# Attention filler: Q and K of a seventh pair computed in the seven-product phase, 13 filler steps a block, the output product one block sooner

## The chip, the cores and the metric

The kernel runs on one core of one Trainium2 chip. The metric is the device time of one execution in microseconds (us), the median of several runs. All of the arithmetic is float32 kept to float32 accuracy by splitting operands into a high and a low part, as told below.

## The reference, cut to what matters

A two-layer decoder trunk over 1024 positions of width 1024: layer 0 mixes with a short gated convolution, layer 1 with dilated attention of 16 heads of 64, and each is followed by a SwiGLU feed-forward. The change touches layer 1's attention only:

```
def dilated_attention_mixer(h, w_qkv, w_out, rel_bias):
    qkv = (h @ w_qkv).reshape(bsz, seq, 3, N_HEADS, HEAD_DIM)
    q, k, v = qkv[:, :, 0], qkv[:, :, 1], qkv[:, :, 2]
    for window, dilation in BRANCHES:                 # (128,1), (512,4), (2048,16)
        o, l = dilated_branch(q, k, v, rel_bias, window, dilation)
        ...
    alpha = jax.nn.softmax(jnp.stack(lses, axis=0), axis=0)
    o = jnp.sum(alpha[..., None] * jnp.stack(outs, axis=0), axis=0)
    return o.reshape(bsz, seq, D_MODEL).astype(h.dtype) @ w_out
...
            x = x + dilated_attention_mixer(h, attn_w_qkv[j], attn_w_out[j], rel_bias)
```

The kernel merges the three branches of a head into one softmax with one common maximum. The result is the same sum.

## The kernel before, in words

**Matmuls.** Every 32-bit operand of the projections is kept as two parts, high and low (`split`, lines 143 and 144: ScalarE rounds the high part, VectorE subtracts to get the low part), and every product of two 128-row tiles is three matmuls (high by high, high by low, low by high). The large products run in a Strassen form: a unit of 2 by 2 blocks takes seven products instead of eight (`Strassen`; its matmuls are lines 572 to 574). A unit needs sums of weight blocks first (`combo`, line 191), sums of partial results behind (`save`, line 578, on ScalarE; `add`, line 582, on VectorE), and 7 x 4 x 3 = 84 matmuls of 512 columns for two weight tiles over all 1024 positions. The plain form (`projections`, its matmuls in `product`, lines 371 to 373) takes 2 x 2 x 8 x 3 = 96 matmuls for the same.

**The seven-product phase.** `QueryKey` computes Q and K for the first `QK_PAIRS` = 6 of the 8 pairs of heads: one unit a pair, in the order of `unit_order`. Each of the four results of a unit goes through `emit` (lines 1140 to 1149): VectorE scales it, ScalarE rounds the high part, VectorE makes the low part, and GpSimd's queue writes both to `kq` in DRAM. Behind the phase come the value tiles of group 0 (`value_tiles`, lines 1512 to 1517: matmuls of 256 columns, 24 to a bank).

**The attention phase.** There are 17 calls of `slot`, called blocks 0 to 16 here. Block n does the scores of head n (`scores`, matmuls lines 1569 and 1570; VectorE adds the bias, lines 1580 to 1611, and keeps the maximum, `m`, lines 1594 to 1620), then the maximum over all partitions on GpSimd (`mb`, line 1623), then the softmax (`softmax`: VectorE subtracts, line 1631; ScalarE takes the exponentials, line 1632), and the product of the exponentials of head n-1 with its values (`values`, matmuls line 1642; ScalarE then copies the two result banks, lines 1665 and 1666). Up to block LAG = 13 ("lagged") the first half of a block interleaves scores with filler, and the second half interleaves the values of head n-1 with filler; the softmax of head n is issued at i = 3 of the second half's eight rounds. From block 14 on, the values of head n-1 run beside the scores of head n.

**Filler.** `fill()` is a generator of independent matmul work, and a block takes a fixed number of its steps, 15: 8 in the first half (4 in block 0, other numbers from block 14 on), the rest spread over the second. The list `FILL` sets its order: values of group 1 and 2, the plain projections of pairs 6 and 7, values of group 3; then `out_product`, the attention's output product over the first four pairs (`AO` = 4), which adds into `X`. A group of value tiles is 40 steps (one step in five only copies a bank and has no matmul; the others have six matmuls of 256 columns), a pair's projections 36 steps (32 with three matmuls of 512 columns), the output product 64 steps (three matmuls of 512 columns each). `take` splits the next weight slabs a little ahead: in `value_tiles` at the steps where j = 1 and b4 is 1 or 2, in `projections` when the second part is taken.

**Operands of the output product.** `load_attended(range(AO))` reads the first four pairs' results (`oin`) back from DRAM through the SyncE queue ahead of block LAG-1 = 12, and the generator `halves` splits one pair into `first` each time it is advanced: in block 12's second half, at i = 4 to 7, behind the softmax. With 15 steps a block, the 192 steps of values and projections end at step 12 of block 12, so the output product begins in the same block.

**Order and space.** The order on each engine is the order of the program (no scheduler). All engines' waits follow from the tiles they share. Full-size tiles come from one pool of 41 pages, 8 PSUM banks serve all matmuls, and the values of a pair are held in a single tile, `vx`.

Of the kernel before, what the change touches and what calls it, by code (L numbers as in the profile page):

```python
# [20 lines left out]
H = 16  # L21
# [20 lines left out]
FFN_PAIRS, FFN_CHUNK = 9, 3  # L42
CONV_PAIRS, CONV_CHUNK, CO = 0, 1, 4
CONV, QK = "conv", "qk"
QK_PAIRS = 6
PAGES = 41
SOFT = 4
FIN0 = 2
AO_WIDE = 5
AO = 4  # L50
LAG = 13
FILL = (("v", 0), ("v", 1), ("v", 2), ("qk", 6), ("qk", 7), ("v", 3))
DEEP_ORDER = (1, 2, 5, 6, 7, 3, 4)


# [44 lines left out]
def trunk(ctx: ExitStack, tc: tile.TileContext, x, gains_in, cwi, ck, cwo, wqkv, wo, relb,  # L100
# [8 lines left out]
    def page(name, dt=F32):  # L109
        return pages.tile([128, 1024], dt, name=name, tag="page", bufs=PAGES)  # L110
# [228 lines left out]
    def add_ffn(i):  # L339
        add_units(i, FT, lambda u, n: (wg, wu)[u % 2][i][u - u % 2 + n])  # L340
        add_down(i, wd[i], FFN_PAIRS, FFN_CHUNK, ("d", i))
# [3 lines left out]
    add_ffn(0)  # L345
    add_units(QK, QK_PAIRS, lambda u, n: wqkv[(KT, 0)[n] + u])
    for kind, g in FILL:
        if kind == "v":
# [47 lines left out]
    class Norm:  # L396
        def __init__(self, gi):
            self.g = gi
            self.h = {}
            self.acc = self.rstd = None  # L400
            self.put_off = None
# [720 lines left out]
    class QueryKey(Conv):  # L1122


        def __init__(self, norm):
            Strassen.__init__(self, QK, norm, QK_PAIRS, 0, 1, 0, None)
            self.waiting, self.ready, self.begun = [], False, iter(())
# [332 lines left out]
    def load_bias(h):  # L1460
        t = scope["pool"].tile([128, L1 + L2], F32, name="bias", tag="bias", bufs=2)
        base = tables.offset + h * G3
        nc.sync.dma_start(t[:, 0:L1], bass.AP(tensor=tables.tensor, offset=base, ap=[[1, 8], [A1, 16], [1, L1]]))
        nc.sync.dma_start(t[:, L1:L1 + L2], bass.AP(tensor=tables.tensor, offset=base + G0,
                                                    ap=[[1, 32], [A2, 4], [1, L2]]))
        return t
# [8 lines left out]
    def attention(norm, qk):  # L1475
# [58 lines left out]
        def load_kq(n):  # L1534

            p, a = divmod(n, 2)
            k, q = qk.kq[p, 1], qk.kq[p, 0]
            rows = lambda t, r: bass.AP(t.tensor, t.offset + r * S, [[S, 64], [1, S]])
            n0, n1 = (slice(64 * i, 64 * i + 64) for i in (a, 1 - a))
            KS[n], QS[n] = page("ka", F32R), page("qa", F32R)  # L1540
            nc.sync.dma_start(KS[n][n0].bitcast(F32), rows(k, 64 * a))
            nc.sync.dma_start(KS[n][n1].bitcast(F32), rows(k, 128 + 64 * a))
            if n <= LAG + 1 and n % 2 == 0 and n:
                load_values(p - 1)
            for m in (n0, n1):
                nc.sync.dma_start(QS[n][m].bitcast(F32), rows(q, 64 * a))
            nc.sync.dma_start(qlo[a][n0].bitcast(F32), rows(q, 128 + 64 * a))

        def classes(n):

            KC[n] = page("kca", F32R)
            for h in range(2):
                nc.scalar.activation(KC[n][:, half(h)], view(KS[n], h * HALF, [[1, 4], [4, 128]]), AF.Copy)
                yield
# [80 lines left out]
        def values(p, a, st):  # L1635
            lf, lh, ld, lp = (st[n] for n in ("lf", "lh", "ld", "lp"))
            acc = [bank(), bank()]
            kd = [[128, 4], [1, 32]]
            b1 = [[32, 16], [1, 8]]

            def mm(ih, off, dims, u, rhs, first=False, last=False):
                nc.tensor.matmul(view(acc[ih], off, dims), vx[:, u, 64 * a:64 * a + 128], rhs,  # L1642
                                 start=first, stop=last)

            for ih in range(2):
                for r4 in range(4):
                    mm(ih, r4 * 32, kd, 8 + r4, view(lf, ih * HALF + r4 * 32, kd), first=r4 == 0)
                    if r4 % 2:
                        yield
            for r4 in range(4):  # L1650
                mm(1, r4 * 32, kd, 12 + r4, view(lh, r4 * 32, kd))
                if r4 % 2:
                    yield
            for j in range(8):
                off = (j % 4) * 8
                mm(j // 4, off, b1, j, view(ld, blk(j), b1), last=False)
                if j:
                    mm(j // 4, off, b1, j - 1, view(lp, blk(j), b1), last=j % 4 == 3)
                yield
            o, z = st["o"], st["z"]  # L1660
            n0 = slice(64 * a, 64 * a + 64)
            z0 = slice(64 - 64 * a, 128 - 64 * a)
            for ih in range(2):
                s = slice(ih * HALF, (ih + 1) * HALF)
                nc.scalar.activation(z[n0, s], acc[ih][z0], AF.Ln)
                nc.scalar.activation(o[n0, s], acc[ih][n0], AF.Copy)
            yield
# [45 lines left out]
        def slot(n, dense, ndense, late=0, hook=iter(())):  # L1713

            def other(k):
                for _ in range(k):
                    next(dense, None)

            p, a = divmod(n, 2)
            if n < H:  # L1720
                new = dict(bias=bias.pop(n))
                sc = scores(p, a, new)
            else:
                sc = iter(())
            if n + 1 < H:
                load_kq(n + 1)
                bias[n + 1] = load_bias(n + 1)
            if n:
                q, b = divmod(n - 1, 2)
                if b == 0:  # L1730
                    OZ[q] = page("o"), page("z")
                old = live.pop(n - 1)
                old.update(o=OZ[q][0], z=OZ[q][1])
                pv = values(q, b, old)
            else:
                pv = iter(())
            extra = later = iter(())
            lagged = n <= LAG
            if n + 1 < H:
                later = classes(n + 1)  # L1740
            if lagged and a and p:
                ending.append(finish(p - 1))
            used = 0
            if lagged:
                for i in range(8):
                    next(sc, None)
                    if n or i % 2:
                        other(1)
                        used += 1
                    if a and ending and i == 0:  # L1750
                        run(ending.pop())
                run(sc)
            else:
                if a == 0 and not late:
                    other(1)
                    used += 1
                for i in range(8):
                    next(sc, None)
                    next(pv, None)
                    next(pv, None)  # L1760
                    if i >= late and i % 2 == 0:
                        other(1)
                        used += 1
                run(sc)
                run(pv)
                if a == 0:
                    extra = finish(p - 1)
                if a == 0 and n < H:
                    load_values(p)
            left = max(ndense - used, 0)  # L1770
            for i in range(8):
                next(pv, None)
                next(pv, None)
                if i == (2 if n > LAG + 1 else 5):
                    attended()
                if not lagged and (i < FIN0 or i > SOFT):
                    next(extra, None)
                if i in (1, 2):
                    next(later, None)
                if i == (3 if lagged else SOFT):  # L1780
                    if n < H:
                        live[n] = new
                        run(softmax(new))
                if i >= SOFT:
                    next(hook, None)
                other(left * (i + 1) // 8 - left * i // 8)
            run(pv)
            run(extra)
# [36 lines left out]
        def fill():  # L1825
            for kind, g in FILL[1:]:
                if kind == "qk":
# [6 lines left out]
        def halves():  # L1834
            for q, t in done.items():
                first[q] = split(t)
                yield

        dense = fill()
        for n in range(H):  # L1840
            if n == LAG - 1:
                done.update(load_attended(range(AO)))
            hook = halves() if n == LAG - 1 else iter(())
            slot(n, dense, 15, 3 if n == H - 2 else 0, hook)
            run(hook)
        acts.update(split_attended(load_attended(range(AO, 7))))
        ensure(ahead_ao)
        slot(H, dense, 15)
        run(dense)
        return acts  # L1850

# [39 lines left out]
    with tc.tile_pool(name="first", bufs=1) as scope["pool"]:  # L1891
# [5 lines left out]
        qk = QueryKey(norm)  # L1897
# [152 lines left out]
```

## Time and profile before

| | |
|---|---|
| median of 3 runs | 2130.8 us (2130.04 to 2131.32) |
| the profiled execution: time | 2129.8 us |
| the profiled execution: span, first to last instruction | 2128.0 us |
| granted TensorE clock, mean | 0.996 |
| TensorE matmuls (PE) busy | 2102.3 us, 99% |
| TensorE weight loads (PEld) busy | 1806.5 us, 85% |
| VectorE (DVE) busy | 1739.8 us, 82% |
| ScalarE (ACT) busy | 1015.7 us, 48% |
| GpSimd (POOL) busy | 234.4 us, 11% |

How to read it: the span is the profiled execution without what lies around it, 1.8 us here. Times in rows are us from the span's start. A matmul's duration in a row overlaps the next one's, so the pitch from start to start is what a matmul costs when TensorE is fed; a busy PE is therefore not yet a fed PE, and its waits have to be looked up. "A <- B" in a view of waits means that engine and line A sat idle until B was done. SPq is the SyncE queue, which issues the loads. Page here means one of the pool's 41 tiles; a page of the profile is named as such.

In the trace, the seven-product phase of Q and K lies at about 972 to 1087 us, block 0 begins at 1110.5, block 1 at 1122.8, block 12 at 1333.0, block 13 at 1358.3, and the last block ends at about 1436.6.

### The profile page before, as it was taken

To read this page: it belongs to the slowest core of one execution; us is meant where nothing else is said; L and a number is where in the kernel's file an instruction comes from. 1 tells how busy PE (TensorE), PEld (TensorE's weight loads), DVE (VectorE), ACT (ScalarE), POOL (GpSimd) and SP (SyncE) were. 2 spreads that over 40 slices of the span, in tenths; PEclk is the share of its full clock that TensorE was granted. 3 is DMA by queue.
4 is the path that set the end of the run, shared out by engine and by line. 5 is a ranking of instruction groups with operands and counts; after the bars stand their busy time and mean duration, and the time that the engine had idled before them with its cause. 6 is when DMAs were issued, how large, how long until landed. Compare 5 with 4: busy or idle time off the path is not lost.

```text
span 2128.0 us, 30922 instructions
## 1 busy us (share of the span) xinstructions
PE 2102.3 (99%) x11082; PEld 1806.5 (85%) x11082; DVE 1739.8 (82%) x3262; ACT 1015.7 (48%) x1861; POOL 234.4 (11%) x335
## 2 busy tenths in 40 slices
PE   9999999999999999999999999999999999999998
PEld 7888888888888888887899999888788888888887
DVE  8898769988888888878967687787998888888876
ACT  7333426443444554445545545554544444456435
POOL 1000000110101000010322322111011101001000
PEclk9999999999999999999999999999999999999999
DMA  7332642323333566351767767745223233358432
GB/s 219 94 94 70 228 134 75 104 100 109 114 101 108 162 208 211 108 168 40 250 208 186 182 182 211 216 164 152 64 85 109 101 108 114 105 195 241 157 95 79
DMA packets 141464, 300.78 MB, mean 141 GB/s; under 512 B 48188, under 2 KB 54414, under 8 KB 141312
## 3 DMA queue, kind: packets, MB, share of 16 engines
q1 hardware_dynamic: 107488, 201.94, 31.5%
q0 software_dynamic: 26192, 82.17, 11.9%
q10 hardware_dynamic: 7632, 14.70, 1.8%
q8 instruction: 88, 1.44, 0.3%
q14 instruction: 64, 0.52, 0.1%
HBM read 208.48 MB, written 82.93 MB: 137 GB/s over the span
## 4 chain that ended last, share of the span: by engine, by line
PE 85%; DVE 7%; ACT 3%; DMA 2%; issue 2%; POOL 1%; SPq 0%; DVEq 0%; ACTq 0%; POOLq 0%
PE bank L574 19%; PE bank L572 19%; PE bank L573 19%; PE bank L373 4%; PE bank L372 4%; PE bank L371 4%; PE bank L664 3%; PE bank L667 3%; PE bank L666 3%; PE bank L1642 2%; POOL mb L1623 1%; PE bank L1512 1%; PE bank L1513 1%; PE bank L1514 1%; DVE w L144 1%
## 5 line engine op out<-in xcount | busy, mean ns | idle before, releaser
L572 PE MATMUL bank<-b,w 128*128 128x512 f32 x1952 | 764.0, 391 | 2.2 <-ACT w L143 1.8
L574 PE MATMUL bank<-b,w 128*128 128x512 f32 x1952 | 762.0, 390 | 3.6 <-DVE w L144 3.5
L573 PE MATMUL bank<-b,w 128*128 128x512 f32 x1952 | 761.4, 390 | 0.4 <-DVE b L883 0.3
L574 PEld LDWEIGHTS bank<-b,w 128*128 128x128 f32 x1952 | 366.9, 188 | 83.9 <-DVE w L144 7.4
L572 PEld LDWEIGHTS bank<-b,w 128*128 128x128 f32 x1952 | 367.2, 188 | 78.9 <-ACT w L143 2.9
L573 PEld LDWEIGHTS bank<-b,w 128*128 128x128 f32 x1952 | 367.1, 188 | 76.3 <-DVE b L883 1.1
L143 ACT ACTIVATE w<-combo 128x512 fp32r<-128x512 f32 (+2 forms) x488 | 249.1, 540 | 230.2 <-DVE combo L191 213.3
L144 DVE TENSOR_TENSOR w<-combo,w 128x512 fp32r<-128x512 f32 (+2 forms) x488 | 277.7, 583 | 37.6 <-ACT w L143 36.9
L578 ACT ACTIVATE part<-bank 128x512 f32<-128x512 f32 x186 | 110.8, 596 | 390.0 <-PE bank L574 386.6
L144 DVE TENSOR_TENSOR w<-raw,w 128x512 fp32r<-128x512 f32 (+2 forms) x342 | 189.5, 576 | 37.5 <-ACT w L143 37.5
L582 DVE TENSOR_TENSOR part<-part,bank 128x256 f32<-128x256 f32 (+1 forms) x366 | 171.5, 500 | 31.1 <-PE bank L574 16.6
L143 ACT ACTIVATE w<-raw 128x512 fp32r<-128x512 f32 (+2 forms) x342 | 166.9, 530 | 44.4 <-PE bank L574 11.5
L371 PE MATMUL bank<-w_hi,w 128*128 128x512 f32 (+1 forms) x400 | 153.4, 384 | 3.8 <-ACT w_hi L143 3.7
L372 PE MATMUL bank<-w_lo,w 128*128 128x512 f32 (+1 forms) x400 | 149.8, 375 | 1.2 <-DVE w_lo L144 1.2
L373 PE MATMUL bank<-w_hi,w 128*128 128x512 f32 (+1 forms) x400 | 149.8, 375 | 0.7 <-DVE w L144 0.7
L493 DVE TENSOR_TENSOR x<-x,bank 128x512 f32<-128x512 f32 (+1 forms) x104 | 66.4, 644 | 62.6 <-PE bank L373 61.4
L802 DVE TENSOR_TENSOR x<-x,bank 128x512 f32<-128x512 f32 x136 | 93.2, 685 | 29.1 <-PE bank L574 29.1
L191 DVE TENSOR_TENSOR combo<-raw 128x512 f32<-128x512 f32 (+1 forms) x172 | 111.7, 649 | 0.0
L371 PEld LDWEIGHTS bank<-w_hi,w 128*128 128x128 f32 x400 | 75.8, 190 | 17.1 <-ACT w_hi L143 3.9
L372 PEld LDWEIGHTS bank<-w_lo,w 128*128 128x128 f32 x400 | 75.9, 190 | 14.9 <-DVE w_lo L144 2.0
L373 PEld LDWEIGHTS bank<-w_hi,w 128*128 128x128 f32 x400 | 75.6, 189 | 14.7 <-DVE w L144 1.6
L565 DVE TENSOR_TENSOR b<-hin,b 128x512 fp32r<-128x512 f32 x126 | 79.7, 689 | 9.3 <-ACT b L564 9.3
(243 smaller groups left out, 3467.1 us busy)
## 6 DMA issues: line engine op xcount, KB each, us to landing
hin<-part SPq DMA_DIRECT2D x126, 256.0 KB
raw<-in_ffn_w_gate SPq DMA_DIRECT2D x44, 512.0 KB
raw<-in_ffn_w_up SPq DMA_DIRECT2D x44, 512.0 KB
part<-sum POOLq DMA_DIRECT2D x72, 256.0 KB, 2.3
raw<-in_ffn_w_down SPq DMA_DIRECT2D x48, 384.0 KB
raw<-in_attn_w_qkv SPq DMA_DIRECT2D x27, 512.0 KB
raw<-in_conv_w_in SPq DMA_DIRECT2D x24, 512.0 KB
part<-part POOLq DMA_DIRECT2D x36, 256.0 KB, 2.4
```

The lines of the kernel that those rows point to most:

```text
L143: nc.scalar.activation(hi, src, AF.Copy)
L144: eng.tensor_tensor(out=lo, in0=src, in1=hi, op=ALU.subtract)
L191: eng.tensor_tensor(out=c, in0=a, in1=b, op=op)
L371: nc.tensor.matmul(b, whi[:, a], ahi[:, s], start=first, stop=False)
L372: nc.tensor.matmul(b, whi[:, a], alo[:, s], start=False, stop=False)
L373: nc.tensor.matmul(b, wlo[:, a], ahi[:, s], start=False, stop=last)
L572: nc.tensor.matmul(b, hi[:, a], bhi, start=start and k == 0, stop=False, skip_group_check=True)
L573: nc.tensor.matmul(b, hi[:, a], blo, start=False, stop=False, skip_group_check=True)
L574: nc.tensor.matmul(b, lo[:, a], bhi, start=False, stop=k == n - 1, skip_group_check=True)
L578: nc.scalar.activation(t, b, AF.Copy)
L582: nc.vector.tensor_tensor(out=t, in0=t, in1=b, op=ALU.add)
L802: nc.vector.tensor_tensor(out=X[n][:, half(h)], in0=X[n][:, half(h)], in1=b, op=ALU.add)
```

## The change

`QK_PAIRS` goes from 6 to 7: pair 6 becomes a seventh unit of the seven-product phase and leaves the filler. The filler loses its 36 steps (220 left of 256), and a block takes 13 steps, named `DENSE`, instead of 15. The values and projections are then 156 steps, which is 12 blocks of 13, so the output product begins with the first step of block 12. Its operands are loaded ahead of block 11 and split in block 11 (LAG-2 instead of LAG-1), at i = 0 to 3 of the second half, ahead of the softmax instead of behind it.

```
-QK_PAIRS = 6
+QK_PAIRS = 7
...
-FILL = (("v", 0), ("v", 1), ("v", 2), ("qk", 6), ("qk", 7), ("v", 3))
+FILL = (("v", 0), ("v", 1), ("v", 2), ("qk", 7), ("v", 3))
+DENSE = 13
...
                 if i in (1, 2):
                     next(later, None)
+                if i < 4:
+                    next(hook, None)
                 if i == (3 if lagged else SOFT):
                     if n < H:
                         live[n] = new
                         run(softmax(new))
-                if i >= SOFT:
-                    next(hook, None)
                 other(left * (i + 1) // 8 - left * i // 8)
...
         for n in range(H):
-            if n == LAG - 1:
+            if n == LAG - 2:
                 done.update(load_attended(range(AO)))
-            hook = halves() if n == LAG - 1 else iter(())
-            slot(n, dense, 15, 3 if n == H - 2 else 0, hook)
+            hook = halves() if n == LAG - 2 else iter(())
+            slot(n, dense, DENSE, 3 if n == H - 2 else 0, hook)
             run(hook)
         acts.update(split_attended(load_attended(range(AO, 7))))
         ensure(ahead_ao)
-        slot(H, dense, 15)
+        slot(H, dense, DENSE)
         run(dense)
```

## The prediction

> **What bounds the kernel now.** I read the page's busy times first, then busy time by stage, then TensorE's (PE's) waits in the attention blocks, then VectorE's (DVE's).
>
> ```profile
> PE 2102.3 (99%) x11082; PEld 1806.5 (85%) x11082; DVE 1739.8 (82%) x3262; ACT 1015.7 (48%) x1861; POOL 234.4 (11%) x335
> ...
> 972.00:1090.00 118.00, 116.78 (x525) 95.11 (x524) 109.50 (x171) 65.97 (x112) 23.12 (x43) 1.00 0.47 162
> 1122.80:1333.00 210.20, 207.11 (x1590) 197.56 (x1589) 160.60 (x287) 114.89 (x163) 57.05 (x52) 1.00 0.72 191
> 1333.00:1358.30 25.30, 21.11 (x151) 19.84 (x150) 16.60 (x28) 16.19 (x25) 5.95 (x6) 0.87 0.53 176
> 1348.30:1352.20 3.90, 0.21 (x2) 0.02 (x1) 1.99 (x3) 3.74 (x7) 0.00 (x0) 0.84 0.01 2
> 1352.20:1357.50 5.30, 4.79 (x14) 3.82 (x15) 3.58 (x3) 4.43 (x7) 2.17 (x4) 0.50 0.39 102
> 1358.30:1436.60 78.30, 77.53 (x496) 69.75 (x495) 62.21 (x106) 40.62 (x62) 10.79 (x5) 1.00 0.65 193
> ```
>
> The columns of a stage are its length, busy time (and count) of PE, weight loads, DVE, ACT and POOL, granted clock, DMA share, GB/s. The stages are the seven-product phase, blocks 1 to 11, block 12, a hole in it (two rows), and blocks 13 to 16. PE is busy nearly everywhere; the exception is block 12, where it is empty for 3.9 us and then at clock 0.50 for 5.3 us.
>
> ```profile
> PE bank L371 <- ACT w_hi L143: 3.7, 1, 3.7
> PE bank L1569 <- ACT o L1666: 2.7, 3, 1.1
> PE bank L372 <- DVE w_lo L144: 1.2, 2, 0.8
> PE bank L1569 <- ACT v L1517: 0.3, 1, 0.3
> ...
> 1352.24 0.79 PE L371 MATMUL bank<-w_hi,w 128*128 128x512 f32 x1 [3.72 <-ACT w_hi L143]
> 1353.50 0.79 PE L372 MATMUL bank<-w_lo,w 128*128 128x512 f32 x1 [0.47 <-DVE w_lo L144]
> 1360.06 0.50 PE L372 MATMUL bank<-w_lo,w 128*128 128x512 f32 x1 [0.77 <-DVE w_lo L144]
> ```
>
> The waits are all of PE's over blocks 0 to 16, the rest its timeline. The hole is the output product's first step (L371): its operand, split from `oin` on ACT behind the softmax, comes when PE has nothing else left to do. The other waits are for PSUM banks that ACT frees late (L1666).
>
> ```profile
> DVE lf L1631 <- POOL mb L1623: 35.3, 11, 3.5
> DVE w_lo L144 <- ACT w_hi L143: 9.3, 4, 3.5
> DVE kq_lo L1148 <- ACT kq_hi L1145: 3.6, 4, 1.3
> DVE lf L1580 <- PE bank L1570: 1.8, 3, 1.0
> DVE ld L1606 <- PE bank L1570: 0.9, 3, 0.4
> DVE lh L1589 <- PE bank L1570: 0.8, 1, 0.8
> ```
>
> These are DVE's waits in blocks 1 to 11. In 210.2 us it waits for PE only 1.8 + 0.9 + 0.8 = 3.5 us. Its other idle time is its own loop: maximum, GpSimd's reduction `mb` (about 3.2 us a block), softmax. So PE and DVE pace these blocks together, each with some 3 us of slack, and filler taken from PE is worth only as much as DVE's loop lets through. That is the main question here.
>
> **The change part by part.** The price of a matmul:
>
> ```profile
> 1430.10 0.39 PE L372 MATMUL bank<-w_lo,w 128*128 128x512 f32 x1
> ...
> 1449.82 0.39 PE L372 MATMUL bank<-o_lo,w 128*128 128x512 f32 x1
> ...
> 1343.10 0.28 PE L1514 MATMUL bank<-w_hi,b 128*128 128x256 f32 x1
> 1343.22 0.28 PE L1512 MATMUL bank<-w_hi,b 128*128 128x256 f32 x1
> ```
>
> Between the first two rows run 87 matmuls of 512 columns back to back: 19.72 / 87 = 0.227 us each. The other two give 0.12 us for 256 columns. A filler step of projections or output product is 3 x 0.227 = 0.68 us, one of values with matmuls 6 x 0.12 = 0.72 us.
>
> *1. The seventh unit* adds 84 x 0.227 = 19.0 us of PE. DVE beside it:
>
> ```profile
> L191 DVE TENSOR_TENSOR combo<-raw 128x512 f32<-128x512 f32 x7 | 4.8, 688 | 0.0
> L144 DVE TENSOR_TENSOR w<-combo,w 128x512 fp32r<-128x512 f32 x17 | 11.7, 685 | 0.1
> L582 DVE TENSOR_TENSOR part<-part,bank 128x512 f32<-128x512 f32 x10 | 6.8, 684 | 2.3 <-ACT part L578 2.3
> ...
> L144 DVE TENSOR_TENSOR w_lo<-raw,w_hi 128x1024 fp32r<-128x1024 f32 x8 | 10.7, 1361 | 9.3 <-ACT w_hi L143 9.3
> L1148 DVE TENSOR_TENSOR kq_lo<-kq,kq_hi 128x512 fp32r<-128x512 f32 x8 | 6.1, 768 | 3.6 <-ACT kq_hi L1145 3.6
> L1140 DVE TENSOR_TENSOR kq<-bank,rstd 128x512 f32<-128x512 f32 x4 | 4.2, 1052 | 0.0
> L1142 DVE SCALAR_TENSOR_TENSOR kq<-bank,rstd 128x512 f32<-128x512 f32 x4 | 2.7, 682 | 0.0
> ```
>
> (mean ns is the number after the busy time.) Four sums, seven splits, three additions, two scalings of K, two of Q and four low parts: 4 x 0.69 + 7 x 0.69 + 3 x 0.68 + 2 x 1.05 + 2 x 0.68 + 4 x 0.77 = 16.2 us, under the 19.0 of PE, so it hides. The cost is at least 19.0. It is at most about 21: DVE is busy 109.5 of 118 us in the phase, and four `b` tiles of block 8 now lie beside a whole further unit in a pool of 41, so splits may wait for a page; 2 us is my estimate, some two of the 0.69 us splits with their ACT halves. I take 19.0. The two weight loads and eight `kq` writes only move.
>
> *2. The filler* loses 32 steps with matmuls, 32 x 0.68 = 21.8 us of PE. By stage, from the step numbers (15n to 15n+14 before, 13n to 13n+12 after; four in five value steps count): block 0 loses 1.6 value steps, 1.2 us. Blocks 1 to 11 go from 74.4 value and 64 projection steps (97.1 us) to 85.6 and 32 (83.4 us), 13.7 us less. Blocks 12 to 16 lose the 9.6 value steps that spilled into block 12, 6.9 us.
>
> *3. Blocks 1 to 11, what is let through.* PE alone: 210.2 - 3.0 (bank waits) - 13.7 = 193.5. DVE alone: 210.2 - 3.5 (its waits for PE) = 206.7. It loses pair 6: four low parts, four scalings, two wide splits, 4 x 0.77 + 2 x 1.05 + 2 x 0.68 + 2 x 1.36 = 9.3, and half of the 3.6 waited for `kq_hi`. It gains the four operand splits in block 11, 4 x 1.36 = 5.4 us, of which 3.5 fill the empty wait for `mb`: 1.9 more. DVE alone is 206.7 - 9.3 - 1.8 + 1.9 = 197.5. The longer decides: DVE, 197.5, a gain of 12.7. Ends: 193.5 (gain 16.7), and 197.5 + 3.5 if DVE still waits for PE as often (gain 9.2).
>
> *4. Block 12's hole.* The operands are split a block earlier, in the wait for `mb`, before ACT's exponentials. The hole goes: 3.9 us, half of the 5.3 us at clock 0.50 (2.65), and the 0.77 wait, 7.3 in all. What is late next is the addition into `X`, which waits for its load from `spill`. The moved loads:
>
> ```profile
> 1300.01 0.54 POOL L1708 DMA_DIRECT2D odram<-o  x1 [4.54 <-DVE o L1707]
> 1297.67 0.47 SPq L1541 DMA_DIRECT2D ka<-kq  x1
> 1313.84 1.26 SPq L1531 DMA_DIRECT2D vx<-vdram  x2
> SPq L1805 <- PE bank L1570: 8.0, 1, 8.0
> ```
>
> On SyncE's queue the four `oin` loads pass ahead of head 12's `ka`, `vx`, `qa`, `ql` and bias loads (`ka` ran at 1297.67). They must wait for the fourth pair's write, issued at 1300.01, and hold that group some 5 us; but its second half of `vx` waits for head 9's values until 1313 anyway, so `qa` behind it is no later. I take nothing. On POOL only `vdram` writes come sooner. `X`'s loads (L1805) waited 8.0 us for a tile's release by the scores (L1570), in block 12's first half; they now stand ahead of it in the program, when `oin`'s four pages are free again. I take nothing.
>
> *5. The tail.* From block 14 on the values of head n-1 follow its softmax at once, and two fewer steps (1.36 us) stand between. At most that is lost again in blocks 15 and 16, 2.8 us; at least nothing. I take 0.5, since DVE is busy only 62.2 of 78.3 us in blocks 13 to 16.
>
> Sum: 19.0 - 1.2 - 12.7 - 7.3 - 6.9 + 0.5 = -8.6 us, against the profiled execution's 2129.8 (span 2128.0): 2121.2. That execution lay 1.0 below the median 2130.8, so the forecast is 2122.2.
>
> **The rivals.**
>
> *PE alone paces (chance 0.16).* DVE's waits for ACT and `mb` shrink as its load does, and part 3 gains 16.7: 2118.2. For it: in eleven blocks PE waits for banks only 3.0 us, though DVE is hardly ever ahead of it. Against it: those waits exist already, with more filler.
>
> *DVE loses more (0.16).* Weight splits now fall on steps 25, 65, 98 and 141, that is at a block's end or first step, where ACT still copies out the values' banks; DVE then stands with the next head's additions queued behind it. The worst wait of this kind is 3.5 us: 4 x 3.5 instead of 9.3 is 4.7 more: 2126.9.
>
> *Slower (0.13): bank waits that halve the clock.* The longest bank wait is 1.1 us now. Each block loses up to 1.4 us of PE work in which ACT could free the banks; if in blocks 2 to 11 lateness adds up over two or three blocks, one wait reaches the 3.7 us after which the clock fell to 0.50 in block 12. Each such hole costs 7.3, and from the second on the gain is gone: 2122.2 + 14.6 = 2136.8. The Trainium skill, "TensorE: Matmul & The Clock Gate", Part 1, states such a gate: after an idle window of about 3.4 us the clock falls to half until a busy window has passed. The rows of block 12 agree, at 3.72 us and 0.50; by that rule waits below it cost only their own length, and then this rival needs holes that no row but block 12's shows.
>
> *The hole only moves (0.08).* If `X` or a weight slab is late in block 12, PE stops there again for as long: 2122.2 + 7.3 = 2129.5, no change.
>
> **How the numbers follow.** A measurement tells about 0.2%, 4.3 us, from no change: below 2126.5 is faster. The forecast case has 0.47. Faster: 0.47 + 0.16 + half of DVE's case = 0.71; same: its other half and the moved hole, 0.16; slower 0.13. Range: 2116.0 (PE alone, with the last bank waits gone) to 2130.0 (the moved hole and half a us of unknown), which leaves out the slower case.
>
> **What the profile after would show.** Right: no PE wait on ACT `w_hi`, no stage at clock 0.50; seven units; blocks 1 to 11 in 195 to 199 us; DVE's waits for PE in them near zero; block 12 about 19 us. Part 3 is wrong if the waits of L1569 for `o` (L1666) exceed some 6 us in all, part 1 if PE waits for splits (L144) among L572 to L574 after the unit before last. The forecast fails if any hole above 3.7 us stands in blocks 1 to 16.

## The result, and the profile after

The changed kernel takes 2134.57 us (2133.47 to 2136.18, 18 runs) against 2130.53 us before on the same chip: a ratio of 1.0018, 95% interval 1.0011 to 1.0025. It is slower by 4 us, just inside what was called no change beforehand, where a gain of 8.6 was forecast and 2130.0 was the top of the range. The profiled execution took 2134.68 us, with a span of 2132.6.

All line numbers are one higher than before, because of the new line `DENSE = 13`. The page's busy times, and then busy time by stage (length, PE, weight loads, DVE, ACT, POOL, clock, DMA share, GB/s): blocks 1 to 11, block 12, and blocks 13 to 16 up to the end of their matmuls.

```profile
PE 2102.0 (99%) x11070; PEld 1805.7 (85%) x11070; DVE 1749.0 (82%) x3274; ACT 1021.5 (48%) x1869; POOL 236.9 (11%) x335
...
1141.90:1347.50 205.60, 196.48 (x1554) 190.04 (x1553) 153.49 (x276) 113.49 (x160) 55.22 (x44) 0.98 0.70 183
1347.50:1370.90 23.40, 20.86 (x127) 18.36 (x126) 22.09 (x35) 12.40 (x18) 5.96 (x6) 0.93 0.71 212
1370.90:1442.00 71.10, 71.10 (x470) 64.70 (x469) 56.90 (x100) 39.81 (x59) 10.80 (x5) 1.00 0.65 190
```

Blocks 1 to 11 have 36 matmul records fewer and 10.6 us less of busy PE than before, yet they are only 4.6 us shorter, and the clock in them is 0.98 where it was 1.00. Block 12 lost 1.9 us where some 6 were expected (from 25.3 to about 19). Here are PE's waits from the seven-product phase to block 16:

```profile
PE bank L1570 <- ACT o L1667: 8.1, 4, 4.0
PE bank L1570 <- ACT v L1518: 3.1, 2, 2.6
PE bank L573 <- ACT w L144: 0.6, 1, 0.6
PE bank L575 <- DVE w L145: 0.5, 1, 0.5
PE bank L1570 <- DVE lf L1581: 0.2, 1, 0.2
```

The hole of before (PE on ACT `w_hi`, 3.7 us) is gone. In its place the scores of the next head (L1570) wait for a PSUM bank, 3.97 us in block 3, 2.56 in block 6, 1.35 in block 10 and 2.53 in block 12. Behind three of the four the clock is halved, for 4.9 us from the end of the wait in block 3 and for 3.4 in the other two:

```profile
1186.70:1191.00 4.30, 4.30 (x20) 4.30 (x21) 3.88 (x10) 4.25 (x7) 2.16 (x4) 0.50 0.56 138
1241.70:1246.00 4.30, 4.13 (x16) 3.57 (x17) 4.26 (x11) 4.22 (x8) 1.64 (x4) 0.62 0.96 295
1317.10:1321.00 3.90, 3.70 (x30) 3.70 (x31) 3.83 (x10) 3.87 (x7) 1.45 (x3) 1.00 0.98 315
1355.00:1358.50 3.50, 3.13 (x10) 2.55 (x11) 3.46 (x9) 3.46 (x7) 1.72 (x4) 0.56 1.04 247
```

Those are the stretches behind the waits of blocks 3, 6, 10 and 12. PE is busy in all of them, but in the first it passes 20 matmuls in 4.3 us, and in the third 30 in 3.9.

**Where the time went.** The ledger is taken from the starts of the blocks in both traces. From block 16 on both kernels run at a fixed distance of 4.6 us, the difference of the spans.

| | expected | measured |
|---|---|---|
| before and in the seven-product phase (block 0 starts at 1130.24, not 1110.47) | +19.0 | +19.8, of which 0.7 stood already ahead of the phase, where executions of the same code differ by as much |
| block 0 | -1.2 | -0.7 |
| blocks 1 to 11 (205.7, not 210.2) | -12.7 | -4.55 |
| block 12 and all behind it | -13.7 | -9.9 |
| sum | -8.6 | +4.6 |

**How the wait of block 3 comes about.** The timeline of ACT, DVE, GpSimd and PE from the end of block 1 to the start of block 3's second half (start, duration, engine, instruction; in brackets the idle time ahead of it and what ended it):

```profile
1165.27 0.59 ACT L1667 ACTIVATE o<-bank 64x512 f32<-64x512 f32 x1
1165.77 1.05 ACT L144 ACTIVATE w_hi<-raw 128x1024 fp32r<-128x1024 f32 x1
...
1166.85 1.23 DVE L145 TENSOR_TENSOR w_lo<-raw,w_hi 128x1024 fp32r<-128x1024 f32 x1 [4.76 <-ACT w_hi L144]
...
1176.21 0.69 DVE L1621 TENSOR_TENSOR m<-m,lp 128x512 f32<-128x512 f32 x1
1177.15 3.22 POOL L1624 PARTITION_ALL_REDUCE mb<-m  x1 [17.06 <-PE bank L1643]
1180.40 1.23 DVE L1632 TENSOR_TENSOR lf<-lf,mb 128x1024 f32<-128x1024 f32 x1 [3.51 <-POOL mb L1624]
...
1186.06 0.59 ACT L1667 ACTIVATE o<-bank 64x512 f32<-64x512 f32 x1
1186.70 0.58 PE L1570 MATMUL bank<-qa,ka 128*128 128x256 f32 x1 [3.97 <-ACT o L1667]
```

A weight split falls on filler step 25, which is the last step of block 1 when a block has 13. Its half on ACT (L144) therefore stands behind the previous head's exponentials and bank copies (L1666, L1667), and its half on DVE (L145) waits for it 4.76 us. DVE's queue runs in order, so the bias additions of block 2 wait behind that; the maximum, `mb`, the softmax, ACT's exponentials and ACT's next bank copies are all late by it, and at 1182.7 PE has nothing left that needs no bank. The second copy of `o` ended 9.8 us after the start of block 3; where it ends no more than 5.8 us after a block's start (blocks 4, 5, 7, 8, 9 and 11 here), PE does not wait for it. The split of step 65, the first step of block 5, does the same to block 6.

**And the wait of block 12.** The same view, blocks 11 and 12:

```profile
1342.87 6.32 DVE L145 TENSOR_TENSOR w_lo<-oin,w_hi 128x1024 fp32r<-128x1024 f32 x4
1343.12 4.05 POOL L1624 PARTITION_ALL_REDUCE mb<-m  x1 [15.82 <-DVE m L1621]
1349.11 1.21 DVE L1632 TENSOR_TENSOR lf<-lf,mb 128x1024 f32<-128x1024 f32 x1
...
1354.71 0.59 ACT L1667 ACTIVATE o<-bank 64x512 f32<-64x512 f32 x1
1355.35 0.57 PE L1570 MATMUL bank<-qa,ka 128*128 128x256 f32 x1 [2.53 <-ACT o L1667]
```

The four operand splits do stand beside `mb`, but they take 6.32 us there, and `mb` takes 4.05 where it takes 3.22 without them. The softmax starts 1.9 us after `mb` has ended, and 2.7 us later than behind a `mb` of 3.22 us and no splits.

### The profile page after: what moved, and what is told of

Read it like the earlier page. It is cut to its first block, busy times and chain, and to the rows that moved or that the text cites. A ratio compares the mean times of both kernels' runs of the same rounds, so it can differ in the third digit from the quotient of the medians.

```text
span 2132.6 us, 30932 instructions
## 1 busy us (share of the span) xinstructions
PE 2102.0 (99%) x11070; PEld 1805.7 (85%) x11070; DVE 1749.0 (82%) x3274; ACT 1021.5 (48%) x1869; POOL 236.9 (11%) x335
## 4 chain that ended last, share of the span: by engine, by line
PE 86%; DVE 6%; issue 3%; ACT 2%; DMA 1%; POOL 1%; DVEq 0%; POOLq 0%; ACTq 0%; SPq 0%
PE bank L575 19%; PE bank L573 19%; PE bank L574 19%; PE bank L372 4%; PE bank L374 4%; PE bank L373 4%; PE bank L1643 3%; PE bank L665 3%; PE bank L668 3%; PE bank L667 3%; PE bank L1570 1%; PE bank L1571 1%; DVE w L145 1%; DVE b L566 1%; PE bank L1513 1%
## 5 line engine op out<-in xcount | busy, mean ns | idle before, releaser
L575 PE MATMUL bank<-b,w 128*128 128x512 f32 x1980 | 771.8, 390 | 5.5 <-DVE w L145 5.3
L573 PE MATMUL bank<-b,w 128*128 128x512 f32 x1980 | 773.9, 391 | 1.7 <-ACT w L144 1.7
L574 PE MATMUL bank<-b,w 128*128 128x512 f32 x1980 | 771.6, 390 | 0.3 <-DVE b L884 0.3
L575 PEld LDWEIGHTS bank<-b,w 128*128 128x128 f32 x1980 | 371.8, 188 | 87.5 <-DVE w L145 10.1
L573 PEld LDWEIGHTS bank<-b,w 128*128 128x128 f32 x1980 | 372.0, 188 | 79.6 <-ACT w L144 2.7
L574 PEld LDWEIGHTS bank<-b,w 128*128 128x128 f32 x1980 | 372.0, 188 | 77.3 <-DVE b L884 1.1
L144 ACT ACTIVATE w<-combo 128x512 fp32r<-128x512 f32 (+2 forms) x492 | 252.1, 542 | 232.5 <-DVE combo L192 207.1
L145 DVE TENSOR_TENSOR w<-combo,w 128x512 fp32r<-128x512 f32 (+2 forms) x492 | 280.9, 585 | 37.6 <-ACT w L144 36.9
L145 DVE TENSOR_TENSOR w<-raw,w 128x512 fp32r<-128x512 f32 (+2 forms) x345 | 193.1, 581 | 40.0 <-ACT w L144 40.0
L144 ACT ACTIVATE w<-raw 128x512 fp32r<-128x512 f32 (+2 forms) x345 | 169.0, 532 | 44.6 <-PE bank L575 12.2
```

The source lines that it names most:

```text
L144: nc.scalar.activation(hi, src, AF.Copy)
L145: eng.tensor_tensor(out=lo, in0=src, in1=hi, op=ALU.subtract)
L573: nc.tensor.matmul(b, hi[:, a], bhi, start=start and k == 0, stop=False, skip_group_check=True)
L574: nc.tensor.matmul(b, hi[:, a], blo, start=False, stop=False, skip_group_check=True)
L575: nc.tensor.matmul(b, lo[:, a], bhi, start=False, stop=k == n - 1, skip_group_check=True)
```

## The experiments

The theory (A in the expectations): the terms of load were right, and the time is lost at three places only, where a split puts itself ahead of a head's additions or softmax (steps 25 and 65, and the operand splits in block 11); each costs its wait and then about as much again at half clock. The rival: with 13 filler steps the blocks are too thin for ACT to free its banks in time, wherever the splits stand. The seventh unit and the hole are checked first, each by itself. Every run has its own runs of the kernel before beside it, 2129.9 to 2130.0 us.

**The unit alone.** The kernel before with one line changed; the filler still computes pair 6 as well, a second time.

```
-QK_PAIRS = 6
+QK_PAIRS = 7
```

> The kernel before with the seventh unit alone: pair 6 is computed in the seven-product phase and, once more, in the filler, which stays as it was (36 steps for pair 6, 15 steps a block). Every theory that keeps part 1 of the prediction expects 84 x 0.227 = 19.1 us more than before: 2149.6, with the waits of blocks 0 to 16 as before, the hole of block 12 included. If the unit itself disturbs what follows (pages, kq writes, DVE's backlog at the start of block 0), it is 21 us or more, and blocks 0 to 3 are longer than before.

Measured: 2150.24 us, ratio 1.0095 (1.0081 to 1.0109), 20.2 us more. Block 0 starts at 1130.48, as in the changed kernel, and PE's waits in the attention blocks are those of before:

```profile
PE bank L371 <- ACT w_hi L143: 3.7, 1, 3.7
...
PE bank L1569 <- ACT o L1666: 2.7, 3, 1.1
```

In the traces the phase is 19.0 us longer (967.87 to 1107.44, and 966.89, not some 972, to 1087.44 before), and another 1.0 us stood ahead of it, where the code is the same. So the unit costs what its 84 matmuls cost, and the waits behind it stay as they were. One thing differs: in block 3 the clock is halved for 3.4 us behind waits of 1.03 and 0.49 us, and the block takes 21.98 us, not 21.03; the last section comes back to it. What the change loses, it loses in the blocks.

**The operands early, alone.** The kernel before (15 steps, six units) with the load and the splits moved as in the change.

```
-            if n == LAG - 1:
+            if n == LAG - 2:
...
-            hook = halves() if n == LAG - 1 else iter(())
+            hook = halves() if n == LAG - 2 else iter(())
...
+                if i < 4:
+                    next(hook, None)
                 if i == (3 if lagged else SOFT):
...
-                if i >= SOFT:
-                    next(hook, None)
```

> The kernel before with only the output product's operands a block sooner: loaded ahead of block 11, split in block 11 at i = 0 to 3 ahead of the softmax. Theory A (the four splits hold up the softmax: beside the reduction mb they took 6.3 us in the changed kernel, where the empty wait is 3.4, so block 11's banks come free some 3 us later than the 3.1 us after the block's end they have now, and PE waits in block 12): the hole of 7.3 goes, a wait of L1569 for o of about 1 us comes, 2124.5. Rival B (the splits are free in the wait for mb, and the wait in block 12 of the changed kernel came from the shorter blocks alone): all of 7.3 is gained, 2123. Rival C (the early splits cost as much as in the changed kernel, 4.8 us): 2128.

Measured: 2124.76 us, ratio 0.9976 (0.9967 to 0.9985). Block 12 falls from 25.3 to 18.3 us: the 7 us of part 4 are there. The splits and PE's waits:

```profile
1324.05 6.32 DVE L144 TENSOR_TENSOR w_lo<-oin,w_hi 128x1024 fp32r<-128x1024 f32 x4
1324.33 4.03 POOL L1623 PARTITION_ALL_REDUCE mb<-m  x1 [12.49 <-DVE m L1620]
...
PE bank L1569 <- ACT o L1666: 2.7, 3, 1.1
PE bank L1642 <- DMA vx<-vdram: 1.8, 1, 1.8
PE bank L1569 <- ACT v L1517: 0.3, 1, 0.3
```

The collision with `mb` is the same here, 6.32 and 4.03 us, and it makes the bank copies 2.3 us later than before (5.4 us after the start of block 12, not 3.1), and PE does not wait for them. In the changed kernel block 11 is late already: `mb` starts 13.2 us after the block's start, here 9.8, and DVE waits there 2.5 us in all for ACT's halves of two narrow weight splits. With that the same collision costs a hole. What is late next was not named in the forecast: `vx`, whose load had been covered by the hole, 1.79 us in block 13. The gain is 5.2 us, not 7. Theory A's time came true, but not its wait in block 12; rival B's 2123 us lies within the interval too.

**The two weight splits moved.** The changed kernel, with the two splits of a value group's second half at its first and third bank and not its second and third: steps 25 and 65 become 20 and 60.

```
-                if j and b4 in (1, 2):
-                    ensure(op_state[1] + b4 - 1)
+                if j and b4 in (0, 2):
+                    ensure(op_state[1] + b4 // 2)
```

> The changed kernel with the value groups' weight splits moved: in value_tiles at b4 0 and 2, not 1 and 2, so that the one that fell on the last step of block 1 falls on the last step of its first half, and the one on the first step of block 5 falls on block 4's second half. Theory A (DVE stands behind ACT: a split issued at a block's edge waits on ACT behind the exponentials and the copies of the values' banks, 4.8 us in block 2, and the lateness passes through mb and the softmax to the banks, with waits of 4.0 us in block 3 and 2.6 us in block 6 and the half clock behind them): the 7.0 - 0.7 us lost in block 3 and 4.7 - 0.4 lost in block 6 go, 10.6 us: 2124. Theory B (13 steps are too few for the loop scores, mb, softmax, bank copies, wherever the splits lie): no change beyond 2 us, 2133 to 2136.

Measured: 2123.62 us, ratio 0.9971 (0.9959 to 0.9982), 11 us below the changed kernel. The stages (blocks 1 to 11, and block 3), and PE's waits:

```profile
1140.73:1336.07 195.34, 192.45 (x1554) 186.65 (x1553) 154.29 (x276) 113.25 (x160) 56.09 (x44) 1.00 0.73 191
1177.61:1194.51 16.90, 16.90 (x148) 16.90 (x147) 12.72 (x26) 10.74 (x15) 5.37 (x5) 1.00 1.00 251
...
PE bank L1570 <- ACT o L1667: 3.8, 3, 2.5
PE bank L1570 <- ACT v L1518: 0.6, 1, 0.6
...
1167.40 1.23 DVE L145 TENSOR_TENSOR w_lo<-raw,w_hi 128x1024 fp32r<-128x1024 f32 x1 [0.49 <-PE bank L1570]
```

Block 3 is 16.9 us long instead of 23.3, block 6 17.45 instead of 21.8: 6.4 + 4.4 = 10.8 us. (Blocks 2 and 12 took 0.7 and 0.5 us more, and this execution reached block 0 1.15 us sooner, where the code is the same.) The last row is the second split of the pair, in block 2, which no longer waits for ACT; the first now stands in block 1. The steps a block has are the same 13, so for blocks 3 and 6 the rival falls: not too little filler, but two splits in the wrong step. The wait that is left, 2.5 us, is block 12's.

**The operand splits spread over four blocks.** The changed kernel, one pair loaded and split in each of the blocks 8 to 11.

```
-            if n == LAG - 2:
-                done.update(load_attended(range(AO)))
-            hook = halves() if n == LAG - 2 else iter(())
+            q = n - (LAG - 1 - AO)
+            if 0 <= q < AO:
+                done.clear()
+                done.update(load_attended([q]))
+            hook = halves() if 0 <= q < AO else iter(())
```

> The changed kernel with the output product's operands loaded and split one pair a block, in blocks 8, 9, 10 and 11, each at i = 0 of the second half, instead of four in block 11. Theory A (four splits of 1.5 us each delay block 11's softmax by 3 us beyond the wait for mb): block 12 loses its wait of 2.5 us and the half clock behind it, 4.8 - 0.5 = 4.3 us: 2130.3; a single split of 1.5 us fits the wait of 3.4. Theory B (13 steps are too few): a wait of about 2 us stays in block 12 and others come in blocks 9 to 11, 2133 to 2137.

Measured: 2132.03 us, ratio 1.0011 (1.0002 to 1.0020): 2.5 below the changed kernel, where 4.3 were expected. The two intervals overlap, so the block lengths of the traces say more.

```profile
PE bank L1570 <- ACT o L1667: 7.5, 5, 3.9
PE bank L1570 <- ACT v L1518: 3.1, 2, 2.5
PE bank L372 <- ACT o L1667: 0.5, 1, 0.5
```

Block 12 falls from 23.4 to 20.5 us, its wait to 0.6 and 0.5, and blocks 3 and 6 keep theirs (3.95 and 2.51). But now `mb` takes 3.76 to 4.13 us in blocks 9 to 11, and blocks 10 and 11 wait 1.90 and 0.76 us: one wide split beside `mb` is enough to lengthen it, and blocks 10 and 11 became 0.5 and 0.7 us longer.

**Both.** The two edits above together.

> The changed kernel with both edits, the value groups' splits moved and the operands split one pair a block in blocks 8 to 11. Theory A (each late split costs the block behind it, and the blocks are independent as long as the lateness of the banks stays under some 5.3 us): the gains add, 2123.6 - 2.5 = 2121.1, with waits of under 2 us in blocks 10 to 12 and the clock at 1.00 throughout. Rival (what is saved in one block is waited for in the next, since 13 steps leave no room): 2123 or more, a wait above 2 us stays in blocks 10 to 12.

Measured: 2122.44 us, ratio 0.9966 (0.9954 to 0.9979), the lowest median of all. The two largest of its waits in the blocks:

```profile
PE bank L1570 <- ACT o L1667: 3.0, 4, 1.9
PE bank L1570 <- ACT v L1518: 0.6, 1, 0.6
...
```

No wait is above 1.9 us and no stretch at half clock is left in the blocks. The difference of 1.2 us from moving the splits alone is within both intervals, so whether the gains add in full cannot be told from the times. In the traces block 12 is 3.4 us shorter than with the splits moved alone (20.47 and 23.88), and blocks 10 and 11 are 0.8 and 0.7 us longer.

**The spread placed where there seemed to be room.** As the last, but with the pairs in blocks 6, 7, 8 and 11, chosen by how early the bank copies had ended there.

```
+            q = {6: 0, 7: 1, 8: 2, 11: 3}.get(n)
```

> The changed kernel with the splits of the value groups moved, and the operands split one pair a block in blocks 6, 7, 8 and 11 (pair 3 alone in block 11). In the run with only the value splits moved, the second bank copy of blocks 6 to 8 ended 4.3, 4.8 and 5.1 us into the next block, of blocks 9 and 10 6.9 and 5.9. Theory A (a split costs only where the lateness is already near 5.3 us): blocks 6 to 8 take one each for nothing, blocks 9 and 10 stay as they are, 2120. Rival (each split beside mb costs its 0.8 to 1.5 us wherever it stands): 2122.

Measured: 2127.68 us, ratio 0.9989 (0.9980 to 0.9998): both missed. DVE's splits in blocks 6 and 7, with ACT's half of the second, and PE behind it:

```profile
1242.18 1.23 DVE L145 TENSOR_TENSOR w_lo<-oin,w_hi 128x1024 fp32r<-128x1024 f32 x1 [2.06 <-DMA odram<-o]
1264.09 1.06 ACT L144 ACTIVATE w_hi<-oin 128x1024 fp32r<-128x1024 f32 x1 [6.15 <-PE bank L1643]
1265.18 1.23 DVE L145 TENSOR_TENSOR w_lo<-oin,w_hi 128x1024 fp32r<-128x1024 f32 x1 [2.69 <-ACT w_hi L144]
1273.06 0.39 PE L1570 MATMUL bank<-qa,ka 128*128 128x256 f32 x1 [2.15 <-ACT o L1667]
```

I had chosen by one resource, the time of the bank copies, and others were not ready. In block 6 DVE waited 2.06 us for the pair's results on their way through DRAM, but inside the wait for `mb`: the softmax began 0.03 us behind `mb`, so this cost nothing. In block 7 ACT, which makes the high half, came late, and the softmax began 4.2 us after `mb` had ended. ACT itself had been idle for 6.15 us, by the view until the values of the head before were done (L1643); why its half had to wait for them, for a free page perhaps, is not shown. Blocks 8 and 9 took 21.5 and 20.6 us, and 17.4 and 18.1 with the value splits moved alone; what block 9 loses was not looked into. As in the change itself, a split whose half on ACT is late holds back a softmax.

**The operand splits beside the scores.** The changed kernel, with the splits at i = 0 to 3 of block 11's first half.

```
+                    if i < 4:
+                        next(hook, None)
...
-                if i < 4:
-                    next(hook, None)
```

> The changed kernel with block 11's four operand splits at i = 0 to 3 of the first half, beside the scores, and not beside GpSimd's mb in the second. This asks what the place beside mb is worth. Theory A' (VectorE and GpSimd get in each other's way: beside mb the four splits take 6.3 us and mb 4.05; elsewhere four take some 4.7 and mb 3.2, but then nothing fills the wait for mb): the softmax of head 11 is late by 4.7 rather than 6.3 - 3.4 = 2.9 us, the wait in block 12 grows from 2.5 to about 4.3, 2136. Rival (the collision with mb is all of the delay): the wait shrinks to about 1 us and the clock stays up, 2131.

Measured: 2139.59 us, ratio 1.0046 (1.0033 to 1.0059). There is no collision (`mb` takes 3.22 us, each split 1.22), but the additions stand behind the splits, `mb` starts 13 us after the last score, and block 12 begins with the longest wait of all:

```profile
1358.35 0.58 PE L1570 MATMUL bank<-qa,ka 128*128 128x256 f32 x1 [5.88 <-ACT o L1667]
```

The time lies beyond both expectations; theory A' had the direction, but put the wait at 4.3 us, and DVE also waited 3.13 us for ACT's half of the first split. So the wait for `mb` is the better place for the splits although they collide with it there.

## Why the prediction was wrong, point by point

**Part 1, the unit: right.** 19.0 expected; the phase is 19.1 us longer in the changed kernel and 19.0 in the run with the unit alone. PE's waits for splits inside the phase came to 1.1 us, as before the change (0.6 and 0.5).

**Part 2, the filler: right as a load.** PE was busy 10.6 us less in blocks 1 to 11 for 13.7 us of steps taken away, but its busy time contains half-clock stretches; with the splits moved the same blocks took 195.3 us, of which PE was busy 192.5, and "PE alone" had been put at 193.5.

**Part 3, what is let through: the step that failed.** The step is "The longer decides: DVE, 197.5": the larger of two totals over eleven blocks, with PE's waits put at nothing. Measured were 205.7 us. With two splits moved it is 195.3 us, of which PE is busy 192.5, and all of the time in blocks 3 and 6; so where the splits stand well, PE's total (193.5) is the one that decides. The sum for DVE took 9.3 us of DVE's work away with pair 6 and left DVE's waits for ACT's high half, which by coincidence are 9.3 us too, as they were. In blocks 1 to 11 of the changed kernel these and two like them are:

```profile
DVE w_lo L145 <- ACT w_hi L144: 8.7, 2, 4.8
DVE kq_lo L1149 <- ACT kq_hi L1146: 4.2, 2, 3.5
DVE w L145 <- ACT w L144: 2.5, 2, 1.9
```

For weights that is 8.7 + 2.5 = 11.2 us, 1.9 more than was left in, and the blocks took 8.2 us more than forecast. What matters is that the 8.7 us come in two pieces, 4.76 in block 2 and 3.91 in block 5, where before it was four of at most 3.5. Each passes through `mb`, the softmax and the bank copies, and PE pays for it a block later: a wait of 3.97 us and one of 2.56, and the half clock behind them, 10.8 us together by the run with the splits moved. That a wait of DVE can become a wait of PE, and a longer loss there, is what a total for each engine does not hold. The signs given beforehand came: waits of L1569 (now L1570) for `o` above some 6 us (8.1), and a hole above 3.7 (3.97).

The prediction had this place as a rival ("DVE loses more"), at 4.7 us and a chance of 0.16, with 3.5 us on each of steps 25, 65, 98 and 141. Steps 25 and 65 cost DVE 4.76 and 3.91 us, and step 141 1.94. Step 98 is not at a block's edge, as was said there, but the eighth of 13 in block 7, and DVE did not wait for it. The rival's place was right, and its price was the wrong one: DVE's wait, not PE's loss.

With the splits moved and spread the change takes 2122.4 us, and 2122.2 had been forecast: blocks 1 to 11 take 196.8 us (197.5) and block 12 20.5 (about 19).

**The slower rival: right that bank waits would halve the clock, wrong in how they arise.** It asked for lateness that adds up over two or three blocks until a wait reaches 3.7 us, and gave it 0.13. No adding up was needed: one split made 3.97 us at once, and waits of 2.56 and 2.53 us halved the clock too. Its 2136.8 us is 2 us from the result, in part by luck: it counted two holes of 7.3 us, and there were three, of 6.4, 4.4 and 3.4 us by the runs without them. What took most of the weight from this rival was that a wait under 3.7 us costs only its own length. The trace before spoke against it already: the wait in block 12 began at 1348.5, and the prediction's row of 3.9 us with a mean clock of 0.84 means that the clock fell at about 1351.0, after 2.4 us of waiting.

**Part 4, the hole: gone, with a wrong price behind it.** The 7 us are real, as the kernel before with the operands early shows (block 12 at 18.3 us; about 19 was given). The mis-sized term is part 3's "5.4 us, of which 3.5 fill the empty wait for `mb`: 1.9 more". The splits take 6.3 us there and not 5.4, and lengthen `mb` by 0.8; the softmax is 2.7 us late, 0.8 more than was counted. And no term held that block 11 is itself later in the changed kernel (`mb` starts 13.2 us after the block's start, 9.8 in the run with the operands early alone). Block 12 came to 23.4 us, and to 20.5 with the splits spread. The moved loads cost nothing that shows in the changed kernel, as said; only in the kernel before with the operands early does `vx` come late (1.79 us).

**Part 5, the tail: a little better than said.** From block 13 on the changed kernel gains 8.0 us, where the spilled steps and the tail came to 6.4. What the other 1.6 are was not looked into.

## What to carry to other kernels

A sum of loads says what a stage can reach, and not what it does: when the number of filler steps in a block changes, write down for every split or copy in the filler which engine's queue it now joins, and behind what, as a step of two engines in order stops both. Price a stall by where it ends: one that reached TensorE in one piece of two microseconds or more was paid twice here, by the wait and by the half clock behind it, and shorter ones close together once were too. And after a hole is filled, look for what it had been covering, and for the slack that is no longer there.

## What was not expected of the hardware

**The clock falls after shorter waits than thought, and their length alone does not decide.** Waits of 1.35, 1.79, 1.90 and 1.91 us were followed by clock 1.00; all from 2.15 up (2.15, 2.51 to 2.56, 3.72 to 3.97 and 5.88) by a half. But with the unit alone 1.03 us and, 0.7 us later, 0.49 (block 3) were followed by a half as well, and the same pair in the kernel before (1.04 and 0.51) was not. The moments of the falls help. In the changed kernel they are 1184.73, 1242.76 and 1355.40, and the distances from the first, 58.0 and 170.7 us, are 17 and 50 times 3.41; the falls of the other traces fit such steps as well, and every stretch at half clock in the blocks lasts 3.4 or 6.8 us. So the clock changes here only at steps of 3.41 us, and what PE was idle between two of these can be counted. Pairs of such pieces, the first with the wait, the second with the clock that followed (two pairs of the changed kernel, blocks 10 and 6, then one of the unit alone, block 3):

```profile
1314.44:1317.85 3.41, 2.06 (x17) 1.85 (x16) 3.41 (x8) 3.36 (x6) 0.55 (x1) 1.00 0.88 277
1317.85:1321.27 3.42, 3.42 (x31) 3.42 (x30) 3.35 (x8) 3.41 (x6) 1.72 (x4) 1.00 0.97 310
...
1239.35:1242.76 3.41, 0.90 (x6) 0.85 (x7) 3.41 (x8) 3.25 (x6) 0.57 (x1) 1.00 0.98 211
1242.76:1246.17 3.41, 3.41 (x13) 2.89 (x12) 3.38 (x8) 3.37 (x6) 1.24 (x3) 0.50 0.99 335
...
1184.43:1187.84 3.41, 1.89 (x14) 1.48 (x13) 3.38 (x10) 3.31 (x7) 0.00 (x0) 1.00 0.96 270
1187.84:1191.25 3.41, 3.41 (x18) 3.41 (x17) 2.74 (x7) 3.26 (x4) 0.00 (x0) 0.50 0.16 46
```

PE is idle for 1.35, 2.51 and 1.52 us in the three first pieces (length less PE's busy time). Over the blocks of all nine traces (two have no fall there, and their steps are counted back from one near 2115 us), a piece at full clock with 1.99 us or more of idle was always followed by a half, and one with 1.47 or less never; between them lie 1.52 (a half) and 1.68 and 1.74 (none). The wait of 1.90 us with the splits spread was cut in two by such a moment, 1.07 and 0.82. So whether a wait of one to two microseconds halved the clock hung on where it fell. This is read from the traces afterwards; no run moved a wait to test it. The Trainium skill, "TensorE: Matmul & The Clock Gate", Part 1, has the clock fall after an idle window of about 3.4 us; here 2.15 us without a matmul was enough. The length agrees with the pieces here, but they need not be idle throughout.

**DVE's splits and GpSimd's reduction slow each other.** `mb` takes 3.22 us alone and 4.03 to 4.05 beside the four splits, and the splits 6.32 us beside it. Without it three of them take 3.50 (in the tail of the kernel with the weight splits moved), which is 4.67 for four, and beside the scores each took 1.22; and in block 12 of the changed kernel a narrow split that mostly takes 0.69 us takes 2.10 beside `mb`:

```profile
1420.37 3.50 DVE L145 TENSOR_TENSOR w_lo<-oin,w_hi 128x1024 fp32r<-128x1024 f32 x3 [0.25 <-ACT w_hi L144]
1363.07 2.10 DVE L145 TENSOR_TENSOR w<-raw,w 128x512 fp32r<-128x512 f32 x1
```

The Trainium skill, "SBUF — State Buffer", section "Who interferes with whom", says that a DVE instruction with both inputs in SBUF contends with GpSimd's reads. The trace agrees that they contend, and shows the price: DVE lost some 1.65 us and GpSimd 0.8, less than if one had stood still for the whole of the other.
